# One input pair loaded later: a sparse 3x3 convolution whose fifth pair of images comes in one transfer

## The chip, the cores and the metric

The kernel runs on one core of a Trainium2 chip. The metric is the device time of one execution in microseconds, as a median of several runs. A core has five engines that run side by side: TensorE (PE, matrix products into PSUM), VectorE (DVE), ScalarE (ACT), GpSimd (POOL) and SyncE (SP, which here only issues transfers). Transfers between HBM and SBUF run on the core's 16 DMA engines; transfers issued by SP go through one queue (q1, "hardware_dynamic" in the profile), those issued by POOL through another (q0, "software_dynamic").

## The reference

The kernel computes a 3x3 convolution with padding 1. The input x is 16 images of 64 channels by 64 x 64 in float32, the weight has 128 output channels and nine tenths of its entries are zero, and the output is 16 x 128 x 64 x 64 in float32.

```
x_pad = np.pad(x, ((0, 0), (0, 0), (pad, pad), (pad, pad)), mode='constant')
output = np.zeros((batch, c_out, h, w), dtype=np.float32)
for b, co, ci, kh, kw in all indices:
    if weight[co, ci, kh, kw] != 0:
        output[b, co] += weight[co, ci, kh, kw] * x_pad[b, ci, kh:kh+h, kw:kw+w]
```

The input is 16.8 MB, the output 33.6 MB.

## The kernel before

The images are worked on in eight pairs: the 64 channels of two images fill the 128 partitions. A pair is cut into four blocks of 16 output rows, so there are N = 32 blocks, k = 0 to 31; pair p has the blocks 4p to 4p + 3. For each block the even and odd output rows are made from three kinds of products, so that some of the work is shared: POOL adds neighbouring rows (`sums`, `fill_sums`), ScalarE copies the odd rows (`odd`, `fill_odd`), POOL copies the even rows (`even`, `fill_even`), each in bf16 with a zero row at the border. TensorE multiplies these with combinations of the weight's taps (`product`, L350), in 30 matmuls per block, all issued from one loop. ScalarE copies the shared product from PSUM (`pc`, L305), and VectorE adds it to the other two (L318, L322) into the output buffer of the pair. Four output buffers are used in turn; the fourth lies in the same memory (`home`) as the first inputs.

Loads: SP issues the weight (L105) and the first 32 rows of the first pair (L108), as float32. All other loads are issued by POOL, which turns float32 into bf16 on the way, so these read twice the bytes that they write. `load(p, i)` (L111 to L113) issues piece i of pair p; `PIECES` gives each pair's pieces as ranges of rows, and each piece has its own semaphore. POOL issues the rest of the first pair at the very start and the pairs 1, 2 and 3 (counted from 0) ahead of its loop (L288). From then on POOL's loop (L290 to L298) goes by blocks: for block k it waits until TensorE has used the buffers of block k - 2, makes `sums` and `even`, and then issues the loads that `WHEN` or `GROUPS` has for that k. POOL works in order, so the place of a load in this loop is also the time from which it can be moved. In `GROUPS` stand the loads of the last pair, which come in parts behind the blocks 18 and 19.

Whoever reads a row waits for the piece that holds it: `source(p, r)` (L140 to L147) looks up the piece's semaphore, `fill` and `fill_sums` wait for it.

Stores: SP waits until VectorE has finished a pair (L334) and issues the store of 4 MB (L335); the pairs 6 and 7 are stored in halves, the very last half behind the loop (L384). SP does nothing else, and the order of its issues is the order of the pairs. VectorE writes pair p into the buffer of pair p - 4, and for that waits for the store of that pair (L315).

Of the kernel before, what the change touches and what calls it, by code (L numbers as in the profile page):

```python
# [22 lines left out]
def kernel(  # L23
# [7 lines left out]
    B, C_IN, H, W = x.shape  # L31
# [6 lines left out]

    PIECES = {p: [(0, H)] for p in range(NP)}
    PIECES[0] = [(HEAD, H)]  # L40
    PIECES[4] = [(0, 28), (28, H)]
    WHEN = {1: (4, 0), 6: (4, 1), 8: (5, 0), 13: (6, 0)}

# [65 lines left out]
    def load(p, i=0):  # L111
        a, b = PIECES[p][i]
        nc.gpsimd.dma_start(out=xs[p][:, a:b, :], in_=pair(p)[:, a:b, :]).then_inc(s_x[p][i], 16)  # L113
# [176 lines left out]
    for k in range(1, N):  # L290
        for fill_in, product in ((fill_sums, 2), (fill_even, 6)):
            if k >= UNROLL:
                wait(g, s_pe, 6 * (k - UNROLL) + product)
            fill_in(k)
        if k in WHEN:
            load(*WHEN[k])
        for group in GROUPS.get(k, ()):
# [124 lines left out]
```

## Time and profile before

| what | us |
|---|---|
| median of 3 runs | 125.27 (125.09 to 125.6) |
| the profiled execution | 125.05 |
| its span, first to last instruction | 123.2 |
| TensorE busy | 109.5 (89%) |
| VectorE busy | 82.6 (67%) |
| POOL busy | 65.7 (53%) |
| ScalarE busy | 54.6 (44%) |
| first store issued | 22.41 |
| last store issued | 113.45 |

The page divides the span into 40 slices of 3.08 us. A digit is the busy share of an engine in tenths. The GB/s row counts the bytes that packets move as they are written, so for a load with a change of type it counts the bf16 bytes. A row of the DMA issues gives a kind of transfer, its size as written, and the time from its issue to its landing. Times within the span are counted from its start.

### The profile page before, as it was taken

How to read it: one execution, taken by the hardware profiler on the slowest of the kernel's cores; microseconds unless marked ns; L12 is line 12 of the kernel's file. 1: busy time of each engine (PE TensorE's matmuls, PEld its weight loads, DVE VectorE, ACT ScalarE, POOL GpSimd, SP SyncE). 2: the span in 40 equal slices, each digit the busy share in tenths (PEclk: the TensorE clock that was granted, in tenths of full speed). 3: DMA queues.
4: the chain of work that ended last, by engine and by line, in shares of the span. 5: the costliest groups of instructions: out<-in, count | busy, mean ns of one | idle time of the engine just before them, and what ended most of it. 6: DMA issues, size and time to landing. Idle time of an engine off the chain costs nothing.

```text
span 123.2 us, 2488 instructions
## 1 busy us (share of the span) xinstructions
PE 109.5 (89%) x983; PEld 56.1 (46%) x983; DVE 82.6 (67%) x74; ACT 54.6 (44%) x79; POOL 65.7 (53%) x92
## 2 busy tenths in 40 slices
PE   5969999999999999999999999999999999993000
PEld 1425555555555555555555555555555555551000
DVE  0576777777777777777777777777777777777000
ACT  4534445555555554444444444455555555530000
POOL 4569555575755556655559975555555565200000
PEclk9999999999999999999999999999999999999555
DMA  3999999999999999999999999999999999999994
GB/s 108 356 225 215 213 213 215 192 391 409 339 340 309 319 322 420 434 298 309 333 431 428 351 367 363 399 350 386 424 419 431 426 436 410 428 426 426 426 428 181
DMA packets 4643, 42.79 MB, mean 347 GB/s; under 512 B 538, under 2 KB 538, under 8 KB 1312
## 3 DMA queue, kind: packets, MB, share of 16 engines
q1 hardware_dynamic: 3008, 34.90, 67.4%
q0 software_dynamic: 1632, 7.87, 31.3%
q14 instruction: 3, 0.02, 0.0%
HBM read 17.07 MB, written 33.55 MB: 411 GB/s over the span
## 4 chain that ended last, share of the span: by engine, by line
PE 83%; DVE 2%; issue 0%; DVEq 0%
PE ps L350 83%; DVE home L322 1%; DVE home L318 1%; DVEq L170 0%
## 5 line engine op out<-in xcount | busy, mean ns | idle before, releaser
L305 ACT COPY pc<-ps 128x1024 f32<-128x1024 f32 x32 | 32.4, 1012 | 51.8 <-PE ps L350 51.8
L350 PE MATMUL ps<-odd,wT 64*128 64x504 bf16 (+1 forms) x384 | 47.2, 377 | 0.0
L350 PE MATMUL ps<-even,wT 64*128 64x504 bf16 (+1 forms) x384 | 47.2, 377 | 0.0
L318 DVE TENSOR_TENSOR o<-ps,pc 128x1024 f32<-128x1024 f32 x24 | 29.4, 1225 | 19.6 <-PE ps L350 19.6
L350 PEld LDWEIGHTS ps<-odd,wT 64*128 64x128 bf16 x384 | 21.6, 94 | 19.9
L350 PEld LDWEIGHTS ps<-even,wT 64*128 64x128 bf16 x384 | 21.6, 94 | 19.9
L322 DVE TENSOR_TENSOR o<-ps,pc 128x1024 f32<-128x1024 f32 x24 | 29.4, 1224 | 0.0
L350 PE MATMUL ps<-sums,wT 64*128 64x504 bf16 (+1 forms) x192 | 26.5, 377 | 1.0 <-PEq L361 1.0
L207 POOL TENSOR_TENSOR sums<-x 128x512 bf16<-128x512 bf16 x16 | 18.5, 1155 | 0.1
L196 POOL COPY even<-x 128x576 bf16<-128x576 bf16 (+1 forms) x16 | 10.4, 650 | 14.6 <-PE ps L350 14.6
L350 PEld LDWEIGHTS ps<-sums,wT 64*128 64x128 bf16 x192 | 10.7, 94 | 11.2 <-issue 1.4
L207 POOL TENSOR_TENSOR sums<-home 128x512 bf16<-128x512 bf16 (+1 forms) x11 | 13.3, 1212 | 2.4 <-DMA home<-in_x_dram 2.4
L318 DVE TENSOR_TENSOR home<-ps,pc 128x1024 f32<-128x1024 f32 x8 | 9.8, 1225 | 6.4 <-PE ps L350 6.4
L196 POOL COPY even<-home 128x576 bf16<-128x576 bf16 (+2 forms) x11 | 6.7, 608 | 8.2 <-PE ps L350 8.0
L187 ACT COPY odd<-x 128x576 bf16<-128x576 bf16 (+1 forms) x16 | 10.6, 661 | 0.0
L322 DVE TENSOR_TENSOR home<-ps,pc 128x1024 f32<-128x1024 f32 x8 | 9.8, 1224 | 0.0
L187 ACT COPY odd<-home 128x576 bf16<-128x576 bf16 (+1 forms) x10 | 6.6, 658 | 0.0
L197 POOL MEMSET even<- 128x64 bf16 x8 | 1.2, 152 | 9.4 <-PE ps L350 9.4
L263 PE MATMUL ps<-idle_rhs 128*128 128x512 bf16 x14 | 4.8, 505 | 1.4 <-DVE idle_rhs L228 1.4
L196 POOL COPY even<-x_last 128x576 bf16<-128x576 bf16 (+2 forms) x5 | 2.7, 556 | 4.2 <-PE ps L350 4.2
L207 POOL TENSOR_TENSOR sums<-x_last 128x512 bf16<-128x512 bf16 x4 | 4.6, 1153 | 0.0
L263 PEld LDWEIGHTS ps<-idle_rhs 128*128 128x128 bf16 x14 | 1.5, 118 | 3.4 <-DVE idle_rhs L228 1.4
(26 smaller groups left out, 25.0 us busy)
## 6 DMA issues: line engine op xcount, KB each, us to landing
out_dram<-o SPq DMA_DIRECT2D x5, 4096.0 KB, 18.8
out_dram<-home SPq DMA_DIRECT2D x1, 4096.0 KB, 20.4
out_dram<-o SPq DMA_DIRECT2D x2, 2048.0 KB, 13.1
out_dram<-home SPq DMA_DIRECT2D x2, 2048.0 KB, 9.8
x<-in_x_dram POOLq DMA_DIRECT2D x3, 1024.0 KB, 16.5
home<-in_x_dram POOLq DMA_DIRECT2D x2, 1024.0 KB, 13.0
home<-in_x_dram SPq DMA_DIRECT2D x1, 1024.0 KB, 5.6
x_last<-in_x_dram POOLq DMA_DIRECT2D x1, 640.0 KB, 14.9
```

Source lines behind the costliest of these rows:

```text
L187: copy or (lambda o, i: nc.scalar.copy(out=o, in_=i)),
L196: copy or (lambda o, i: nc.gpsimd.tensor_copy(out=o, in_=i)),
L197: zero or (lambda o: nc.gpsimd.memset(o, 0.0)),
L207: engine.tensor_tensor(out=sums[k % UNROLL], in0=src[:, q0 : q0 + ROWS : 2, :], in1=src[:, q0 + 1 : q0 + ROWS : 2, :], op=ADD,).then_inc(s ...
L263: t.matmul(idle_ps, idle_rhs[:, 0:128], idle_rhs, start=True, stop=True)
L305: a.copy(out=pc[k % 3], in_=ps[0]).then_inc(s_pc, 1)
L318: v.tensor_tensor(out=o[:, :, r0 : r0 + ROWS : 2, :], in0=ps[1], in1=pc[k % 3], op=ADD).then_inc(s_free, 1)
L322: v.tensor_tensor(out=o[:, :, r0 + 1 : r0 + ROWS : 2, :], in0=ps[2 + k % 2], in1=pc[k % 3], op=ADD).then_inc(s_out, 1)
L350: mm = t.matmul(into[:, n, :, c_lo:c_hi], tap(g, kw, n), src[q, i : i + HALF, c_lo + kw - 1 : c_hi + kw - 1], start=(m == 0), stop=(m == l ...
```

## The change

The fifth pair (pair 4) was loaded in two pieces: the rows 0 to 27 behind block 1, the rows 28 to 63 behind block 6. Now all its 64 rows come in one transfer behind block 6. The sixth pair (pair 5), which was loaded behind block 8, is loaded behind block 9. The seventh pair (behind block 13) and the last pair stay where they were. No other line is changed; the lines below it stand one line higher.

```
-    PIECES[4] = [(0, 28), (28, H)]
-    WHEN = {1: (4, 0), 6: (4, 1), 8: (5, 0), 13: (6, 0)}
+    WHEN = {6: (4, 0), 9: (5, 0), 13: (6, 0)}
```

## The prediction

> **What bounds the kernel now.** I read the page's 40 slices first, the chain of waits second, the timelines of SP and POOL third, and the DMA queues in short windows last.
>
> ```profile
> PE   5969999999999999999999999999999999993000
> DMA  3999999999999999999999999999999999999994
> GB/s 108 356 225 215 213 213 215 192 391 409 339 340 309 319 322 420 434 298 309 333 431 428 351 367 363 399 350 386 424 419 431 426 436 410 428 426 426 426 428 181
> HBM read 17.07 MB, written 33.55 MB: 411 GB/s over the span
> PE 83%; DVE 2%; issue 0%; DVEq 0%
> out_dram<-home SPq DMA_DIRECT2D x2, 2048.0 KB, 9.8
> x<-in_x_dram POOLq DMA_DIRECT2D x1, 448.0 KB, 16.8
> ```
>
> The chain of waits names TensorE for 83%, and that misleads. TensorE ends at 111.9 us, the last VectorE addition at 113.2, and the span goes on to 123.2. The DMA row stands at 9 from the second slice to the end, TensorE's row or not. The GB/s row seems to contradict this with 213 in slices 3 to 8, but a load writes bf16 and reads f32: its printed bytes are half of those read. 213 printed is 426 read, which is the pace of the stores in slices 33 to 39 (426 to 428). All traffic is 17.07 + 33.55 = 50.62 MB; from the first packet (1.97) to the last data (about 121.6) that is 423 GB/s, so the 16 engines hardly ever stand still. The transfers set the end: work moved between two busy times costs nothing, and every moment without queued transfers is added to the end.
>
> The timeline of SP (start, duration; 22.41 is the first of three issues merged into one row), then that of POOL:
>
> ```profile
> 0.95 0.39 SPq L105 DMA_DIRECT2D w_sb<-in_weight_dram  x1
> 22.41 26.31 SPq L335 DMA_DIRECT2D out_dram<-o  x3
> 106.69 0.37 SPq L335 DMA_DIRECT2D out_dram<-home  x1
> 113.45 0.37 SPq L384 DMA_DIRECT2D out_dram<-home  x1
> ```
>
> ```profile
> 4.18 0.55 POOL L113 DMA_DIRECT2D x<-in_x_dram  x1
> 9.55 0.57 POOL L113 DMA_DIRECT2D x<-in_x_dram  x1
> 25.04 0.57 POOL L113 DMA_DIRECT2D x<-in_x_dram  x1
> 31.52 0.57 POOL L113 DMA_DIRECT2D x<-in_x_dram  x1
> 54.27 1.15 POOL L207 TENSOR_TENSOR sums<-x 128x512 bf16<-128x512 bf16 x1
> ```
>
> The store issued at 106.69 lands 10.8 us later, at 117.5 (9.8 is the median of two, the other is the last one's 8.9). So when the last store is issued at 113.45 the engines still have some 4 us of older work, and the last store ends late by that backlog, not by TensorE.
>
> The place that the change touches is the change-over from loading to storing. The fourth pair's load (issued 4.18) lands by 23.6, the first engine's share at 23.0; in the packet records its data end between 22.7 and 23.3, 22.95 in the mean over the engines. The first store is issued at 22.41. Between them lies the piece issued at 9.55. The queues (packets, MB, share) in 22.4 to 25.0, then 25.0 to 25.5:
>
> ```profile
> q0 software_dynamic: 133, 0.45, 100.0%
> ...
> q1 hardware_dynamic: 10, 0.16, 78.0%
> q0 software_dynamic: 25, 0.05, 57.6%
> ```
>
> No packet of the store runs before 25.0; until then the 28 rows keep the engines full.
>
> **The change, part by part.**
>
> *Removed: the load of rows 0 to 27 at 9.55.* POOL saves one issue of 0.57 us. The sums of block 2 start that much earlier, but the next copy already waits 1.42 us for TensorE, and TensorE runs from 7.96 without a break at 3.24 us a block. Worth nothing. What matters is what the queue lacks: 28 rows are 128 x 7,168 B = 0.917 MB read, 2.1 us at 430 GB/s, in the trace 2.4 us (22.95 to 25.35). After the change the engines are out of work at 22.95 in the mean. SP still issues the first store at 22.41, since that waits for block 3's last addition (ends 22.38). The gap lasts until the store's first packets, and the trace of before never shows a store meeting empty engines. Bounds:
> - from below, the weight load, which met empty engines: issued 0.95, first packet 1.97, 16 more packets by 2.2. That is 1.02 us to the first and about 1.2 in the mean: 23.6, a gap of 0.65 us.
> - from above, the store of before: 25.0 to 25.9, mean 25.4, a gap of 2.45 us, if it was not ready earlier.
> - between them, a trace of its coming: in 23 to 24 the loads move 201 GB/s printed, in 24 to 25 only 158, at the same full share, and each packet takes 0.36 to 0.5 us where 0.29 is usual. The slow packets begin at 23.5 to 24.3, 1.1 to 1.9 us after the issue. I take this as the store's descriptors reaching the engines: 24.0, a gap of 1.05 us.
>
> I take 1.05: it is the only row of this very store, and lies near the weight load's.
>
> *Credit at the same place.* The slow stretch goes with the piece: 2 x 201 = 402 and 2 x 158 = 316 GB/s read, against 430, lose 0.07 + 0.27 = 0.34 us in these two microseconds. Bounds 0 (the loss comes back elsewhere) and 0.34. I take 0.34.
>
> *Moved: the 28 rows join the load behind block 6 (25.04).* The same bytes run beside stores instead of alone. Beside stores the engines are as busy: in 30 to 36 the shares are 64.0% and 37.9%, together 102%. One packet per partition instead of two: 0.286 + 0.360 us becomes 0.625, 8 per engine, at most 0.17 us gained; packets overlap by more than that, so I take 0.05, bounds 0 and 0.17. When is it there? The load issued at 25.04 has its first packets at 29.5 to 30.3, behind store packets already queued; 8 load packets alternating with 8 store packets (0.62 us each) end near 40. POOL first reads that pair at 54.27, 14 us later: no wait.
>
> *Moved: the sixth pair's load from behind block 8 (31.52) to behind block 9 (34.8).* POOL issues it (0.57 us) ahead of the sums of block 10, which TensorE wants at 40.4; behind these POOL sits idle 1.42 us anyway. It follows the fifth pair's packets in the same queue and ends near 49 or 50 (48.1 before); first read at 65.8. The load queue was empty from 48 to 52.5 in the trace, so the 0.9 MB of extra loading is caught up there, and the seventh pair (47.73) and the last pair (63.94 on, landed 89.6, wanted 93.2) keep their times. SP's queue is passed by nothing: its issues wait for VectorE alone.
>
> *Sum.* +1.05 - 0.34 - 0.05 = +0.65 us, all of it at the end, since nothing behind 26 us has an idle moment to give. The profiled execution took 125.05 (span 123.2 and 1.85 around it): 125.7. It is 0.22 under the median of the runs, so the median to expect is 125.27 + 0.65 = 125.9.
>
> **The rivals.** Half a per cent, 0.63 us, is about what the measurement can tell from no change.
>
> *The store is not ready before 25.2 (B).* Then the gap is 2.45, less 0.34 and 0.05: +2.05, 127.3. For it: the second store, issued at 35.38, shows its first sure packets at 38.6, again about 3 us later. Against it: both met engines full of loads, and a load issued into a running store also waits 4.5 us, which looks like waiting behind what is already fetched; and the weight load took 1.02.
> The Trainium skill (DMA: Bandwidth & Descriptors, Queues, rings and completion order) says that each engine goes round-robin between the queues that have work, a packet at a time. By that rule a ready store would have mixed with the loads at once, so a store that shows nothing before 25.0 was not ready, and the time is B's; the trace agrees once both queues run (101 and 98 packets in 30 to 36), but not at a start, as the load issued at 25.04 shows.
>
> *The gap is nearly covered (C).* The store comes as soon as the weight load did: 0.65 - 0.34 - 0.05 = +0.26, 125.5, no difference that can be told. For it: the only row of an SP transfer on empty engines. Against it: its packets are 2,304 B and its descriptors half as many.
>
> *Faster (D).* One transfer instead of two, and no slow change-over: if the store's packets start before 23.34 on average (22.95 + 0.34 + 0.05) the change gains; at a gap of zero, with the whole 0.17, it is -0.51, 124.8. Speaking against it: 23.34 is 0.93 us after the issue, less than any row.
> The Trainium skill (same page, Specifications) gives about 0.6 us to the first byte of a transfer that SP issues; by it the store starts at 23.0 and the sum is 0.06 - 0.39 = -0.33, 124.9. The trace's 1.02 disagrees, and decides.
>
> *Late data (E).* If the bigger load pushes the last pair's landing (89.6) past 93.2, TensorE waits. It needs a shift of 3.6 us, and the 4 us of older work behind which the last store waits cover as much again; a shift of 9 us would give 125.9 + 1.4 = 127.3. The empty load queue in 48 to 52.5 speaks against any shift.
>
> **How the numbers follow.** My forecast (A, 125.9, own range 125.5 to 126.3) 0.50; B 0.22; C 0.20; D 0.04; E 0.04. Slower by over 0.5% (above 125.9): B, E and half of A, 0.51. Faster by over 0.5% is beyond the bound of D, which takes 0.03 from D for what I have not seen; within 0.5%: C, the other half of A and the rest of D, 0.46. The range runs from 125.3, inside C, to 127.4, just above B; outside lie D, some of C, and the top of B and E.
>
> **What would show it.** In the changed trace: no packet in a stretch from about 23.0 to 24.0, with the DMA share there well under 1 in a half-microsecond window; the first store's packets from 24.0 instead of 25.2; then a full share until the end; the load at 25.04 landing near 40 and no wait of POOL or ScalarE for a DMA behind the first block; the last store landing as much later as the gap is long, less 0.4. I am wrong if the share never falls (C, D), if the first store again starts 2.7 us after its issue (B), if TensorE shows a new idle stretch (E), or if the end moves by something other than the gap.

## The result and the profile after

The changed kernel takes 126.77 us (median of 6 runs, 126.7 to 128.08), the kernel before 125.46 us beside it. The medians differ by 1.31 us, 1.0%. The ratio of the averages is 1.0118, with a 95% interval of 1.0071 to 1.0165; one run of 128.08 us raises it. The change makes the kernel 1.0 to 1.2% slower, clear of the scatter. The profiled execution of the changed kernel took 126.79 us with a span of 124.9, 1.7 us more than the span before.

The rows of the page by slices, the HBM row, and the rows of the first sections that answer to those of before:

```profile
DMA  3999999899999999999999999999999999999994
GB/s 96 364 222 212 218 215 215 310 420 310 323 296 199 299 331 346 393 310 299 373 435 414 341 355 387 378 353 428 420 425 425 441 425 401 422 438 430 425 422 184
HBM read 17.07 MB, written 33.55 MB: 405 GB/s over the span
PE 82%; DVE 2%; issue 0%; DVEq 0%
out_dram<-home SPq DMA_DIRECT2D x2, 2048.0 KB, 11.6
```

The DMA row shows one 8, in slice 8, where the kernel before had a 9: that is the gap which was forecast, and it is small. The GB/s row has more to say. Slices 10 and 13 (counted from 1; about 28 to 31 and 38 to 41 us) fell from 409 to 310 and from 309 to 199. The stores of 2 MB from `home` now take 11.6 us to land in the median, 9.8 before: the last one ends behind a longer backlog.

The timeline of SP, and of POOL with the two loads that were moved:

```profile
22.41 26.31 SPq L334 DMA_DIRECT2D out_dram<-o  x3
113.45 0.37 SPq L383 DMA_DIRECT2D out_dram<-home  x1
```

```profile
25.04 0.57 POOL L112 DMA_DIRECT2D x<-in_x_dram  x1
34.77 0.57 POOL L112 DMA_DIRECT2D x<-in_x_dram  x1
54.27 1.16 POOL L206 TENSOR_TENSOR sums<-x 128x512 bf16<-128x512 bf16 x1
```

These rows stand at the same times, to 0.01 us, as in the kernel before, but for the sixth pair's load, which was moved from 31.52. The fifth pair is first read at 54.27, as before, and the first and the last store are issued when they were. Only the transfers are slower.

Where they lost it is found by counting bytes, with the bytes of q0 (the loads) doubled, since a load reads twice what it writes. The DMA queues of the kernel before in 28 to 32 and in 38 to 42 (packets, MB, share of 16 engines):

```profile
q1 hardware_dynamic: 83, 1.36, 80.1%
q0 software_dynamic: 34, 0.16, 19.1%
...
q0 software_dynamic: 67, 0.51, 60.6%
q1 hardware_dynamic: 49, 0.67, 40.2%
```

The changed kernel in the same two windows:

```profile
q1 hardware_dynamic: 64, 1.05, 82.3%
q0 software_dynamic: 18, 0.15, 17.6%
...
q0 software_dynamic: 68, 0.43, 63.8%
q1 hardware_dynamic: 31, 0.49, 29.3%
```

Before: 1.36 + 2 x 0.16 = 1.68 MB and 0.67 + 2 x 0.51 = 1.69 MB; 4 us at 430 GB/s are 1.72 MB, so nothing is missing. After: 1.35 MB in both. Each window lacks some 0.34 MB, 0.8 us, and the two together are the change. In the first window the engines are nominally as busy as ever (82.3 + 17.6 = 99.9%): the packets of the store, 0.61 us each before and later, take up to 1.2 us between 29 and 31. The busy share shows nothing of this.

From the packet records I work out the lost time of a stretch: its length less its bytes (spread over each packet's time, loads doubled) at 430 GB/s. The table gives this for the profiled execution of each kernel, in us, and the time of the first store's first packet, in us from the span's start (its issue lies between 22.04 and 22.48 in all of them). Medians are of all runs, and each ratio is against the kernel before on the same chip; the ratios leave out the few runs of any kernel that were over 1.5% slower than its fastest.

| kernel | median | ratio (95%) | lost 22-27 | lost 28-35 | lost 36-42 | store's first packet |
|---|---|---|---|---|---|---|
| before | 125.46 | | 0.37 | 0.04 | 0.06 | 25.17 |
| changed | 126.77 | 1.0118 (1.0071, 1.0165) | 0.35 | 0.86 | 0.89 | 23.32 |
| sixth pair back | 126.46 | 1.0073 (1.0040, 1.0107) | 0.32 | 0.79 | 0.50 | 23.12 |
| sixth pair later alone | 125.64 | 1.0007 (0.9973, 1.0041) | 0.56 | 0.04 | 0.38 | 25.38 |
| 8 rows early | 125.78 | 1.0046 (1.0010, 1.0081) | 0.05 | 0.89 | 0.33 | 23.41 |
| two pieces behind 6 | 127.25 | 1.0148 (1.0100, 1.0196) | 0.33 | 0.84 | 0.98 | 23.22 |
| shifted engines | 126.74 | 1.0105 (1.0059, 1.0150) | 0.06 | 0.77 | 0.85 | 23.03 |
| rest behind 7 | 125.61 | 1.0013 (0.9980, 1.0047) | 0.63 | 0.01 | 0.46 | 25.42 |
| 16 rows early | 125.35 | 0.9998 (0.9968, 1.0027) | 0.03 | 0.24 | 0.52 | 23.88 |
| whole pair behind 5 | 126.76 | 1.0102 (1.0068, 1.0136) | 1.52 | 0.10 | 0.02 | 25.42 |
| 28 rows of the sixth pair | 125.17 | 0.9982 (0.9950, 1.0014) | 0.43 | 0.05 | 0.05 | 25.15 |
| 12 rows early | 125.63 | 1.0016 (0.9981, 1.0052) | 0.03 | 0.49 | 0.54 | 23.53 |
| whole pair behind 7 | 126.76 | 1.0085 (1.0032, 1.0138) | 0.49 | 0.72 | 0.85 | 23.37 |
| 18 rows of the sixth pair | 125.11 | 0.9963 (0.9934, 0.9992) | 0.02 | 0.22 | 0.05 | 24.07 |

Between 42 and 120 us no stretch of 2 us loses more than 0.1 in any of them. Behind 120 us the engines end at uneven times, which cost the profiled execution with 28 rows of the sixth pair 0.6 us more than that of the kernel before. A profile is one execution: that of the kernel before took 125.05 us, 0.4 under its median, and the four kernels with 28 rows ahead, alike up to 25 us, lose 0.37 to 0.63 in 22 to 27. So in that column differences of 0.3 us tell nothing, and as much is to be expected between these sums and the medians.

### The profile page after: what moved, and what is told of

Same layout as the page of the kernel before. It is cut to its first block, busy times and chain, and to the rows that moved or that the text cites. A ratio compares the mean times of both kernels' runs of the same rounds, so it can differ in the third digit from the quotient of the medians.

```text
span 124.9 us, 2486 instructions
## 1 busy us (share of the span) xinstructions
PE 110.3 (88%) x983; PEld 56.9 (46%) x983; DVE 82.6 (66%) x74; ACT 54.7 (44%) x79; POOL 65.2 (52%) x91
## 4 chain that ended last, share of the span: by engine, by line
PE 82%; DVE 2%; issue 0%; DVEq 0%
PE ps L349 82%; DVE home L317 1%; DVE home L321 1%; DVEq L169 0%
## 5 line engine op out<-in xcount | busy, mean ns | idle before, releaser
L262 PE MATMUL ps<-idle_rhs 128*128 128x512 bf16 x14 | 5.5, 556 | 1.4 <-DVE idle_rhs L227 1.4
## 6 DMA issues: line engine op xcount, KB each, us to landing
out_dram<-home SPq DMA_DIRECT2D x2, 2048.0 KB, 11.6
```

Source lines behind the costliest of these rows:

```text
L262: t.matmul(idle_ps, idle_rhs[:, 0:128], idle_rhs, start=True, stop=True)
```

## The experiments

**The sixth pair back behind block 8.** From the changed kernel:

```
-    WHEN = {6: (4, 0), 9: (5, 0), 13: (6, 0)}
+    WHEN = {6: (4, 0), 8: (5, 0), 13: (6, 0)}
```

> The changed kernel, but the sixth pair's load is back behind block 8; the fifth pair still comes in one transfer behind block 6. In the changed kernel the engines lose 0.85 us in 28 to 32 (where the fifth pair's load starts) and 0.84 us in 38 to 42 (where the fifth pair's load has ended, and the sixth pair's load and the second store have not begun). Dry theory (the second loss comes of the later issue of the sixth pair's load, so that neither queue has anything ready): the loss in 38 to 42 goes, the one in 28 to 32 stays; about 0.8 us under the changed kernel, 0.5 us over the kernel before. Step theory (the 16 engines run in step since they all begin the first store at once, and in step every start of a second queue costs): both losses stay wherever a start falls; within 0.2 us of the changed kernel. Gap theory of the prediction (only the empty time at 23 counts): no change against the changed kernel, 1.3 us over the kernel before.

Measured: 126.46 us, 0.3 us under the changed kernel (their medians; not run side by side). The loss in 28 to 35 stays (0.79), that in 36 to 42 falls from 0.89 to 0.50. The dry theory has the direction but only half of the size; the missing rows cost about 1.0 us without any later sixth pair.

**The sixth pair later, alone.** From the kernel before:

```
-    WHEN = {1: (4, 0), 6: (4, 1), 8: (5, 0), 13: (6, 0)}
+    WHEN = {1: (4, 0), 6: (4, 1), 9: (5, 0), 13: (6, 0)}
```

> The kernel before, with only the sixth pair's load moved from behind block 8 to behind block 9; the 28 rows stay in the first run. Dry theory: the load of rows 28 to 63 ends at 38.0, the sixth pair's load, issued at 34.8 with 4.6 us to its first packet, begins at 39.4, the first store ends at 37.9: the engines are short of work between 38 and 40, a loss of 0.5 to 0.9 us, so 0.5 to 0.9 us over the kernel before. Step theory: the engines are out of step as in the kernel before, no loss; within 0.2 us of it. Gap theory: the same as the kernel before.

Measured: 125.64 us, ratio 1.0007 (0.9973 to 1.0041). The loss in 36 to 42 appears (0.38, against 0.06), and none in 28 to 35. In the time nothing can be told from no change; the dry theory's 0.5 to 0.9 us is too much.

**Eight rows early.** From the changed kernel:

```
+    PIECES[4] = [(0, 8), (8, H)]
-    WHEN = {6: (4, 0), 9: (5, 0), 13: (6, 0)}
+    WHEN = {1: (4, 0), 6: (4, 1), 9: (5, 0), 13: (6, 0)}
```

> The changed kernel, but 8 of the 64 rows of the fifth pair are loaded behind block 1 (0.6 us of loading), the other 56 behind block 6; sixth pair behind block 9. The 8 rows fill the measured gap (22.95 to 23.4). Gap theory: back to the kernel before, 1.3 us under the changed kernel. Dry theory: only the gap's 0.4 us goes, the loss in 38 to 42 stays: 0.8 to 1.0 us over the kernel before. Step theory: 16 engines end the 8 rows a few tenths apart, so they begin the first store out of step and the losses in 28 to 32 and 38 to 42 shrink: within 0.4 us of the kernel before.

Measured: 125.78 us, 1.0 us under the changed kernel and 0.4 over the kernel before. The gap is gone (0.05 lost in 22 to 27), the loss in 28 to 35 is not (0.89). The queues in 28 to 32:

```profile
q1 hardware_dynamic: 67, 1.10, 84.1%
q0 software_dynamic: 16, 0.11, 13.7%
```

1.10 + 2 x 0.11 = 1.32 of 1.72 MB. That sinks the gap theory: a kernel with no empty time at 23 still loses the 0.8 us at 29. The time fell as far as the step theory had said, but of the two losses that it expected to shrink only the one in 36 to 42 did (0.89 to 0.33), and the dry theory had expected that one to stay.

**Two pieces, both behind block 6.** From the changed kernel (the loop issues each load that `WHEN` lists):

```
+    PIECES[4] = [(0, 28), (28, H)]
-    WHEN = {6: (4, 0), 9: (5, 0), 13: (6, 0)}
+    WHEN = {6: ((4, 0), (4, 1)), 9: ((5, 0),), 13: ((6, 0),)}
...
-        if k in WHEN:
-            load(*WHEN[k])
+        for piece in WHEN.get(k, ()):
+            load(*piece)
```

> The changed kernel, but the fifth pair comes in the two pieces of the kernel before (rows 0 to 27, rows 28 to 63), both issued behind block 6; sixth pair behind block 9. It tells whether the size of the packets matters (3,584 and 4,608 B instead of 8,192 B). Size theory: the loss in 28 to 32 goes, as in the kernel before, where the load starting there has packets of 4,608 B; 0.8 us under the changed kernel. Step, dry and gap theory: within 0.3 us of the changed kernel.

Measured: 127.25 us, 0.84 lost in 28 to 35. Smaller packets do not help where the rows are missing from the first run.

**Half of the engines shifted by half a packet.** From the changed kernel:

```
+    shift = sbuf("shift", [8, 2, 2048], BF16)
...
+        if k == 1:
+            for j, n in enumerate((2048, 16)):
+                src = pair(4)[0:8].rearrange("c h w -> c (h w)")[:, 0:n]
+                nc.gpsimd.dma_start(out=shift[:, j, 0:n], in_=src).then_inc(s_spare, 16)
...
-    wait(g, s_spare, 16 * 2)
+    wait(g, s_spare, 16 * 4)
```

> The changed kernel with two useless loads into a buffer of their own behind block 1: 8 partitions of 8,192 B read (half a packet time, 0.3 us, on 8 of the 16 engines) and 8 partitions of 64 B on the other 8. Half of the engines then begin the first store 0.3 us later, half a period of the 0.61 us packets; the store begins at 23.4 to 23.7 as in the changed kernel and the fifth pair's load is issued at the same time. Step theory (the loss of 0.85 us in 28 to 32 comes of 16 engines running in step): that loss goes or falls below 0.4 us, 0.5 to 0.8 us under the changed kernel. Lead theory (the loss comes whenever the load is issued well after the store has begun, in step or not): the loss stays at 0.7 to 0.9, the time is that of the changed kernel to 0.3 us more.

Measured: 126.74 us. The queues of this kernel in 28 to 32:

```profile
q1 hardware_dynamic: 56, 0.92, 72.5%
q0 software_dynamic: 27, 0.22, 26.3%
```

0.92 + 2 x 0.22 = 1.36 MB, as in the changed kernel. How far the engines run in step can be worked out from the ends of the store's packets within their period of 0.615 us (1 is all 16 in step, 0 is spread evenly); over the two periods up to 28 us it is 0.43 here and 0.87 in the changed kernel. So the edit took the engines only half out of step: their first store packets spread over about half a microsecond, not 0.17. The loss is nearly the same (0.77 against 0.86). The same measure in the other runs goes further against the step theory: with 12 rows early it is 0.15 and the loss 0.49, in the kernel before 0.28 and the loss 0.04. No run has the engines evenly spread with nothing ahead of the store.

**The rest of the rows behind block 7.** From the kernel before:

```
-    WHEN = {1: (4, 0), 6: (4, 1), 8: (5, 0), 13: (6, 0)}
+    WHEN = {1: (4, 0), 7: (4, 1), 8: (5, 0), 13: (6, 0)}
```

> The kernel before, with only the load of rows 28 to 63 moved from behind block 6 (25.0) to behind block 7 (28.3), the sixth pair behind block 8 as before. The engines are out of step and the first store begins at 25.2. Step theory: no loss where this load begins (32 to 34), the time of the kernel before within 0.3 us. Lead theory: the load is now issued 3 us after the store's first packets, in the kernel before 0.2 us ahead of them, in the changed kernel 1.6 us after: a loss of 0.7 to 0.9 us in 31 to 35, 0.7 to 0.9 us over the kernel before.

Measured: 125.61 us, no difference that can be told from the kernel before. The load now begins at 32 to 33, 7 us into the store, and 31 to 35 moves 1.34 + 2 x 0.18 = 1.70 of 1.72 MB:

```profile
q1 hardware_dynamic: 82, 1.34, 79.2%
q0 software_dynamic: 39, 0.18, 21.9%
```

The lead theory falls too: a load may come as late as it likes behind a store that was itself queued behind loads.

**Sixteen rows early.** From the kernel before:

```
-    PIECES[4] = [(0, 28), (28, H)]
+    PIECES[4] = [(0, 16), (16, H)]
```

> The kernel before with 16 instead of 28 rows in the first run (1.2 us of loading), the other 48 behind block 6, sixth pair behind block 8. The loads end near 24.2 and the first store begins then, 0.8 us ahead of the load's issue. Lead theory: a loss of 0.3 to 0.8 us in 28 to 32. Step theory: by then the engines are spread over more than a packet time, the loss is below 0.3 us and the time is that of the kernel before within 0.3 us.

Measured: 125.35 us, ratio 0.9998. The loss in 28 to 35 is down to 0.24; the change-over costs 0.03 instead of 0.37; 0.52 is lost in 36 to 42 instead. That is 0.79 in all against 0.47 for the kernel before, but in the times no difference shows.

**The whole pair behind block 5.** From the changed kernel:

```
-    WHEN = {6: (4, 0), 9: (5, 0), 13: (6, 0)}
+    WHEN = {5: (4, 0), 8: (5, 0), 13: (6, 0)}
```

> The changed kernel with the fifth pair's load behind block 5 (21.8) instead of block 6, sixth pair behind block 8. The load is issued 0.6 us ahead of the store, about when the fourth pair's packets end. Lead theory: no loss where the load begins; the load's packets fill the gap or mix with the store; 0.8 to 1.3 us under the changed kernel. Step theory: store and load begin together in step, a loss of 0.3 to 0.9 us stays before 30.

Measured: 126.76 us. In 22 to 27 the queues moved 2 x 0.70 + 0.07 = 1.47 of 2.15 MB:

```profile
q0 software_dynamic: 102, 0.70, 93.4%
q1 hardware_dynamic: 4, 0.07, 3.1%
```

Load and store, issued 0.6 us apart into engines just running dry, cost 1.5 us at once, and next to nothing in the later two places. Both theories of that round expected less. By the order of issue all 64 rows lie ahead of the store here, so rows ahead are not enough by themselves: in this kernel the load's own records start only at 22.96, 0.7 us after the store's issue.

**28 rows of the sixth pair early, the fifth pair whole.** From the kernel before:

```
-    PIECES[4] = [(0, 28), (28, H)]
-    WHEN = {1: (4, 0), 6: (4, 1), 8: (5, 0), 13: (6, 0)}
+    PIECES[5] = [(0, 28), (28, H)]
+    WHEN = {1: (5, 0), 6: (4, 0), 8: (5, 1), 13: (6, 0)}
```

> The kernel before, but the 28 rows of the first run are rows of the sixth pair (behind block 1); the fifth pair comes whole behind block 6, the rest of the sixth behind block 8. So the first store arrives behind 1.9 us of load packets as in the kernel before, and the load that begins beside it has the packets of the changed kernel (8,192 B). Empty-engine theory (the loss of 0.85 us in 28 to 32 follows from the first store arriving at engines with little or no loading left: 0 rows 0.85, 8 rows 0.78, 16 rows 0.15, 28 rows 0): no loss in 28 to 32, the time of the kernel before within 0.3 us. Packet theory (the loss comes of the size of the load's packets: 8,192 B 0.85 and 0.77, 7,168 B 0.78, 6,144 B 0.15, 4,608 B 0): 0.7 to 0.9 us in 28 to 32, 0.6 to 0.9 us over the kernel before.

Measured: 125.17 us, ratio 0.9982 (0.9950 to 1.0014). Its queues in 28 to 32 and in 38 to 42:

```profile
q1 hardware_dynamic: 70, 1.15, 68.1%
q0 software_dynamic: 32, 0.26, 31.2%
...
q1 hardware_dynamic: 78, 1.03, 61.6%
q0 software_dynamic: 73, 0.32, 38.9%
```

1.15 + 2 x 0.26 = 1.67 and 1.03 + 2 x 0.32 = 1.67 of 1.72 MB: no loss in either place, with the fifth pair in one transfer and with the packets of the changed kernel. The packet theory falls. One transfer for the pair is harmless. This kernel differs from the one with the sixth pair back behind block 8 only in 28 early rows of the sixth pair, and the loss in 28 to 35 falls from 0.79 to 0.05: that too little loading lies ahead of the first store is what costs.

**Twelve rows early.** From the kernel before:

```
-    PIECES[4] = [(0, 28), (28, H)]
+    PIECES[4] = [(0, 12), (12, H)]
```

> The kernel before with 12 rows in the first run (0.9 us of loading, to about 23.9), the other 52 (packets of 6,656 B) behind block 6, sixth pair behind block 8. Empty-engine theory: between 8 rows (0.78 us lost in 28 to 32) and 16 (0.15): 0.2 to 0.7, 0.1 to 0.6 us over the kernel before. Packet theory: the same order, 0.3 to 0.7.

Measured: 125.63 us, which can't be told from the kernel before; 0.49 lost in 28 to 35. With 0, 8, 12, 16 and 28 rows ahead the loss is 0.86, 0.89, 0.49, 0.24 and 0.04.

**The whole pair behind block 7.** From the changed kernel:

```
-    WHEN = {6: (4, 0), 9: (5, 0), 13: (6, 0)}
+    WHEN = {7: (4, 0), 9: (5, 0), 13: (6, 0)}
```

> The changed kernel with the fifth pair's load behind block 7 (28.3) instead of block 6, sixth pair behind block 9. If the loss is paid once, when loads first mix with a store that began at empty engines, it moves with the load to 32 to 35 and stays 0.7 to 0.9 us; if it belongs to the time around 29 (the tenth of a store's 16 packets per engine) it stays in 28 to 32 or goes. Time within 0.4 us of the changed kernel in the first case.

Measured: 126.76 us. The loss moves with the load: the queues in 30 to 34 carry 1.31 + 2 x 0.07 = 1.45 of 1.72 MB, while 28 to 31 is full.

```profile
q1 hardware_dynamic: 89, 1.31, 94.3%
q0 software_dynamic: 9, 0.07, 8.9%
```

It is paid when loads first mix with the store, not at a fixed time.

**18 rows of the sixth pair early.** As the run with 28, with the split at 18:

```
-    PIECES[5] = [(0, 28), (28, H)]
+    PIECES[5] = [(0, 18), (18, H)]
```

> As the run with 28 rows of the sixth pair in the first run and the fifth pair whole behind block 6, but 18 rows instead of 28. Empty-engine theory: 1.35 us of loading lie ahead of the store, more than the 1.2 us (16 rows) with which 0.15 us was lost in 28 to 32; the loss of 0.3 us at the change-over in 24 to 26 shrinks as with 16 rows; the first store lasts until the second is there, so none in 36 to 42. About 125.0 us, 0.2 to 0.4 us under the kernel before. If the fifth pair's larger packets cost after all when fewer rows are ahead: 0.5 us or more over the kernel before.

Measured: 125.11 us against 125.49, ratio 0.9963 (0.9934 to 0.9992): a little faster than both kernels. It loses 0.02 at the change-over, 0.22 in 28 to 35 and 0.05 in 36 to 42, 0.3 in all where the kernel before loses 0.5.

## Why the prediction was right or wrong

The time, 126.77, lies within the range (125.3 to 127.4), and the direction was right. The forecast was +0.65 us and +1.31 was measured, and the sum that led to it was wrong in its terms. That the range holds the time is luck: its upper part stood for the cases B and E, and neither of them happened.

**What bounds the kernel** held. TensorE, VectorE, POOL and SP keep their times in every row compared above, and the end moves by what the transfers lose: 1.65 us more are lost between 22 and 60 us (2.19 against 0.54), the span grew by 1.7.

**The gap, +1.05, was mis-sized.** The first store's first packet came at 23.32, 0.91 us after its issue, the 16 engines' first packets at 23.38 in the mean. The gap is 0.43 us, not 1.05. That lies below even the lower bound (0.65, case C) and just above the case D (0.39). The queues of the changed kernel in 22.4 to 23.3, then in 23.3 to 23.8:

```profile
q0 software_dynamic: 24, 0.07, 41.4%
...
q1 hardware_dynamic: 16, 0.26, 127.5%
q0 software_dynamic: 1, 0.00, 0.3%
```

All 16 engines begin the store within half a microsecond. I had taken the slowed load packets at 24 to 25 as the coming of the store's descriptors, and the weight load's 1.02 us only as the lower bound; the weight load was the nearest row, and still too long. With the credit of 0.34 the change-over comes out even: 0.35 lost there after, 0.37 before.

**B was wrong, and it is clear why.** The store of the kernel before was ready long before 25.17: its first packet tracks the end of the loading ahead of it, 23.41 with 8 rows, 23.53 with 12, 23.88 with 16, 25.17 with 28, and 23.32 with none. A store waits behind the load packets that are already there.

The Trainium skill (DMA: Bandwidth & Descriptors, Queues, rings and completion order) has each engine go round-robin between queues that have work, draining a whole packet before it switches, and gives a packet as typically 9 to 17 descriptors. The prediction took such a packet to be one record of the trace. A load of one piece has 128 large records, 8 for each of the 16 engines. If a record is one descriptor, which no run here shows, a store that waits for a whole piece does not speak against that rule; what does is the load of rows 28 to 63 in the kernel before, whose 8 records of 0.36 us on an engine spread over 8 us beside the store. The same page's Specifications give about 0.6 us to the first byte of a transfer that SP issues. Measured here are 0.91 us for the store and 1.02 us for the weight load from the start of the issue, and 0.51 and 0.63 us from its end, so the prediction's verdict that the trace disagrees hangs on where the time is counted from.

**"Nothing behind 26 us has an idle moment" is the step that failed.** I had costed the moved 28 rows at -0.05, since beside stores the engines are as busy, and the sixth pair's move at nothing. Both rested on the busy share, and the busy share stays at 99.9% in 28 to 32 while the throughput falls to 1.35 of 1.72 MB. In its place the runs showed two losses of 0.8 us each. The first (28 to 35) belongs to the missing rows: it is 0.7 to 0.9 us when the first store meets engines with 0.6 us of loading left or less, 0.49 with 0.9 us and 0.24 with 1.2 us, and it is paid when the next load begins beside that store. The second (36 to 42) comes where the first store has ended and the load queue runs alone until the second store's first packets. The changed kernel in 38 to 40, and the run with 28 rows of the sixth pair:

```profile
q0 software_dynamic: 51, 0.29, 89.9%
q1 hardware_dynamic: 1, 0.00, 0.1%
```

```profile
q1 hardware_dynamic: 34, 0.51, 60.5%
q0 software_dynamic: 24, 0.14, 34.7%
```

In the second kernel the first store, issued as ever but begun later and mixed with larger load packets, lasts until the second store is there, and nothing is lost. The other runs bear this out: in nine kernels, the changed one among them, the first store ended 1.1 us or more (up to 5.3) ahead of the second's first packet, and they lose 0.33 to 0.98 in 36 to 42; in four kernels the two lie at most 0.4 us apart or overlap, and they lose 0.02 to 0.06. The exception is the sixth pair later alone, which loses 0.38 without such a pause. No run changes the pause by itself, so this second cause is argued, not shown.

The later sixth pair is a part of this loss, 0.3 to 0.4 us in the two runs that move it alone, since its load, issued at 34.77, had no packet ready when the fifth pair's ended near 39. In the time that part shows as 0.3 us from the changed kernel's side and not at all from the other.

**Late data (E)** did not occur: no wait of POOL or ScalarE for a load behind the first block, and TensorE ran without a break from 7.97.

A slip that changes nothing: the store pace of 426 to 428 GB/s holds for the slices 35 to 39; slice 33 has 436 and slice 34 has 410.

What stays open is what the engines do in the slow 0.8 us. The packet records show packets of the running queue taking twice their time (1.2 us for 0.61), and in the run with the whole pair behind block 5 up to three times (2.0 us for 0.62), just ahead of the other queue's first packets. That would fit engines reading ahead for the new queue, which a store that was queued behind loads would have had done already, but no run here shows the reading itself. Packet size and the time between the two issues were tried and are not it, and how far the engines run in step does not order the losses.

## What to carry to other kernels

When transfers set the end, look at bytes per microsecond in each stretch, with converted loads counted at what they read; a DMA share of 100% can hide a fifth of the throughput. In this kernel it paid to issue the first store while loads were running and 1.2 us or more of further loading was queued, and to have each store last until the next one is there: 18 rows of a later pair (1.35 us) did both, for 0.4% under the kernel that was there before. Whether the 1.2 us hold elsewhere no run here shows. Too little loading ahead of the first store may cost more at the next mixing than in the gap itself, and even without a gap, so judge a change of their order by the whole stretch that follows.

## What the runs showed of the hardware that was not expected

A store issued into running loads waits for those already queued (first packet 0.93 us after its issue with 8 rows ahead, 1.22 with 12, 1.46 with 16, 2.76 with 28, 0.91 with none), so there is no fixed delay. Where a second queue begins beside one that began on empty or nearly empty engines (0 or 8 rows ahead), the 16 engines lose 0.7 to 0.9 us of throughput at a full busy share; behind 1.2 us of loading 0.24, behind 2.1 us 0.04. A load and a store issued 0.6 us apart on engines just running dry cost 1.5 us.
